# The MLP of a four-layer fp32 trunk on one core: products in program order, high weight tiles first, and a lead that alternates between two blocks

## The chip, the core and the metric

The kernel runs on one core of one Trainium2 chip. The metric is the device time of one execution in microseconds (us). The engines speak through semaphores: PE is TensorE (matmul), ACT is ScalarE, DVE is VectorE, POOL is GpSimd, and SP issues most of the DMAs. Each works through its own instructions in the order in which they stand.

## The reference, cut to what matters

Two layers on 512 tokens of width 1024; each is a mixer (MLA in the first, GLA in the second) followed by an MLP:

```python
x = x + mix
x = x + sq_relu_mlp(rms_norm(x, norm_mlp[i]), mlp_w_up[i], mlp_w_down[i])

def sq_relu_mlp(xn, w_up, w_down):          # w_up 1024 x 4096, w_down 4096 x 1024
    hid = jnp.square(jax.nn.relu(xn @ w_up))
    return hid @ w_down
```

At the end stands one more RMSNorm. The change concerns the two MLPs and the norm ahead of each.

## The kernel before

**Arithmetic.** Every fp32 operand is split into a high and a low fp32r tile (`split`, L108 to L113): ACT copies `src` to `hi` (L110), which rounds, and DVE takes `lo = src - hi` (L113). A product is three matmuls (`mm3`, L118 to L120): high weight by high input, high weight by low input, low weight by high input. `piece` (L143) splits a weight tile; its tiles `wh` and `wl` have three buffers each.

**The products.** Both matmuls of the MLP are cut once in each of three ways (tokens in halves of TH = 256, input width and output width in halves), and seven products are made from sums of the parts where eight would be plain (Strassen's scheme in Winograd's form). The names are 11 and 21 (plain leading part, plain trailing part), T1 to T4 (inputs that are sums of parts of x), and 22. For the up projection the sums of x are made once, by `QuadNorm.pair` (L281), in the output projection ahead of the MLP: for each k of 0 to 3 one ACT operation (L287), four DVE operations (L288 to L291) into a `raw` tile, and a split into `T{k}h` and `T{k}l`. The sums of the weights are made in place on DVE, ahead of each product that needs one (L884, L899, L905, L912).

**Up blocks.** The 4096 hidden columns come in NB = 8 blocks of 512. `up_block(b)` gives the steps s1 (product 11), s5 (T1), s2 (21), s6 (T2), s3 (22), s7 (T3), s4 (T4); block 0 has them in the order 11, 21, T1, T2, 22, T3, T4, behind an s0 that splits its first two weights during the output projection. A product here is 24 matmuls of 128x128 by 128x256: four k, two column groups j, three each, into one PSUM bank (tag `u`, three buffers). The results build on each other in PSUM: T2, T3 and T4 of a block add into one bank (`b2`, tag `seed`, one buffer), which begins as a copy of product 11 (L873); after T3 DVE reads that bank (L915) before T4 may add to it; after T1 and after T2 ACT copies the banks to `mt` tiles (L888, L902). `finish` (L840, L841) multiplies by the norm's 1/rms (`rstd`) and squares. `rstd` is made by `Norm.finish` (L251): a mean by PE (L253), Ln and Exp on ACT, three steps on DVE (L216, L218, L219).

**Down blocks.** `down_block(s)` makes seven products for every pair of up blocks (all but the last pair): 48 matmuls each, in two halves with a `piece` each, into two PSUM banks (tag `d`). The steps of up and down alternate.

**The order.** A scheduler at build time orders each engine's instructions by dependence and priority; so a product's matmuls may stand between those of another. Two calls bind it: `tc.keep_in_program_order(i)` keeps an instruction where the program has it, and `with tc.issue_after(i)` puts the instructions of a block behind `i` on i's engine.

**The lead.** The output projection's last step runs `nxt.pair(3)` (L785). Then `mlp` runs the first two steps of blocks 0 and 1 (L1099 to L1103): 11(0), `begin()` with the norm's mean and four DVE subtractions of x (L1080), 21(0), 11(1), 21(1); the number in brackets is the block. Then come the other steps of block 0, then those of block 1, and so on. Block 1's first weights come as one 1 MB load (L824) into a tile of the pool `down_w`, all others as 512 KB loads (L829) into `raw` tiles of the pool `up` (five buffers).

## Time and profile before

| | |
|---|---|
| median of 3 runs | 1093.47 us (1093.22 to 1094.63) |
| the profiled execution's own time | 1092.46 us |
| its span (first to last instruction) | 1090.7 us |
| busy: PE, DVE, ACT | 1065.7, 892.1, 641.0 us |
| granted clock of PE, mean | 0.996 |
| HBM read, written | 105.69 MB, 2.10 MB |

How to read the profile: rows of the timeline have a start, a duration, engine, line, operation, what is written from what, shapes and a count; square brackets give the idle time ahead and what ended it. Buffer numbers are left out of tile names. Matmuls are pipelined: their durations overlap, and the distance from start to start is the rate. A line is often a helper's, so that L110 and L113 are all splits.

### The profile page before, as it was taken

The page shows a single profiled execution, that of the slowest core. Times are in us where ns is not written, and L with a number is a line of the kernel's source. Part 1 is how long each engine was busy: PE and PEld are TensorE (multiplying, and loading weights), DVE is VectorE, ACT ScalarE, POOL GpSimd, SP SyncE. Part 2 cuts the span into 40 slices and gives each one's busy share as a digit, 9 for nine tenths or more (in the row PEclk, how much of TensorE's full clock was granted, in tenths as well). Part 3 has the DMA queues.
Part 4 walks back from the last instruction along what each step waited for, and adds up shares of the span by engine and source line. Part 5 has one row for each costly group of instructions (what it writes and reads, how often), then busy time and mean ns, then how long its engine had stood idle before and what let it go on. Part 6 is the DMA issues. An engine that isn't in the chain of part 4 may idle for free.

```text
span 1090.7 us, 17825 instructions
## 1 busy us (share of the span) xinstructions
PE 1065.7 (98%) x7322; PEld 981.1 (90%) x7322; DVE 892.1 (82%) x1210; ACT 641.0 (59%) x934; POOL 46.6 (4%) x78
## 2 busy tenths in 40 slices
PE   8999999899999999999999999999999999999997
PEld 6788888889999999998788888887999999999986
DVE  6789878899899899977565655678899899799865
ACT  6577655555667677654334735655565666766734
POOL 6400000000000000030000000000000000000000
PEclk9999999999999999999999999999999999999999
DMA  7312113633433422251222222125424424522312
GB/s 215 87 49 78 29 32 92 198 97 117 149 104 98 155 97 97 78 190 42 53 73 78 78 78 63 53 78 173 132 65 132 141 78 133 167 71 94 134 41 78
DMA packets 99057, 108.93 MB, mean 100 GB/s; under 512 B 8112, under 2 KB 73920, under 8 KB 98976
## 3 DMA queue, kind: packets, MB, share of 16 engines
q1 hardware_dynamic: 96960, 106.57, 31.0%
q10 hardware_dynamic: 1952, 1.21, 0.4%
q8 instruction: 57, 0.93, 0.4%
q0 software_dynamic: 64, 0.02, 0.1%
q14 instruction: 24, 0.20, 0.1%
HBM read 105.69 MB, written 2.10 MB: 99 GB/s over the span
## 4 chain that ended last, share of the span: by engine, by line
PE 87%; DVE 8%; ACT 2%; issue 1%; DMA 1%; SPq 0%; ACTq 0%; DVEq 0%
PE ps L118 27%; PE ps L120 27%; PE ps L119 26%; DVE wl L113 2%; PE ps L135 2%; PE ps L1345 2%; ACT wh L110 1%; DMA wraw_ckv<-in_mla_w_in_dram 1%; DVE raw L1000 1%; DVE raw L884 1%; DVE h L113 0%; PE ps L1382 0%; PE ps L666 0%; DVE raw L912 0%; PE ps L667 0%
## 5 line engine op out<-in xcount | busy, mean ns | idle before, releaser
L110 ACT ACTIVATE wh<-raw 128x1024 fp32r<-128x1024 f32 x210 | 221.3, 1057 | 177.4 <-PE ps L119 135.9
L113 DVE TENSOR_TENSOR wl<-raw,wh 128x1024 fp32r<-128x1024 f32 x210 | 254.4, 1218 | 25.4 <-ACT wh L110 24.9
L120 PE MATMUL ps<-h,wl 128*128 128x256 f32 x672 | 188.4, 280 | 2.6 <-DVE wl L113 2.5
L118 PE MATMUL ps<-h,wh 128*128 128x256 f32 x672 | 187.9, 280 | 0.0
L119 PE MATMUL ps<-h,wh 128*128 128x256 f32 x672 | 187.8, 280 | 0.0
L120 PEld LDWEIGHTS ps<-h,wl 128*128 128x128 f32 x672 | 126.5, 188 | 3.8 <-DVE wl L113 3.8
L118 PEld LDWEIGHTS ps<-h,wh 128*128 128x128 f32 x672 | 126.3, 188 | 0.0
L119 PEld LDWEIGHTS ps<-h,wh 128*128 128x128 f32 x672 | 126.3, 188 | 0.0
L118 PE MATMUL ps<-set,wh 128*128 128x512 f32 x232 | 91.4, 395 | 1.3 <-ACT set L243 1.3
L119 PE MATMUL ps<-set,wh 128*128 128x512 f32 x232 | 90.8, 391 | 1.0 <-DVE set L244 1.0
L120 PE MATMUL ps<-set,wl 128*128 128x512 f32 x232 | 90.6, 390 | 0.0
L110 ACT ACTIVATE wh<-wraw 128x1024 fp32r<-128x1024 f32 x41 | 43.0, 1056 | 73.9 <-PE ps L120 41.5
L118 PE MATMUL ps<-wh,set 128*128 128x512 f32 x144 | 59.7, 414 | 0.0
L841 ACT ACTIVATE q<-q 128x512 f32<-128x512 f32 x64 | 40.1, 627 | 32.0 <-DVE q L840 31.9
L113 DVE TENSOR_TENSOR wl<-wraw,wh 128x1024 fp32r<-128x1024 f32 x41 | 50.0, 1222 | 10.6 <-ACT wh L110 10.5
L113 DVE TENSOR_TENSOR h<-q,h 128x1024 fp32r<-128x1024 f32 x42 | 51.2, 1218 | 7.5 <-ACT h L110 7.5
L120 PE MATMUL ps<-wh,set 128*128 128x512 f32 x144 | 56.4, 391 | 0.0
L119 PE MATMUL ps<-wl,set 128*128 128x512 f32 x144 | 56.2, 391 | 0.0
L119 PEld LDWEIGHTS ps<-set,wh 128*128 128x128 f32 x232 | 43.6, 188 | 11.0 <-DVE set L244 2.2
L118 PEld LDWEIGHTS ps<-set,wh 128*128 128x128 f32 x232 | 43.5, 188 | 11.0 <-ACT set L243 2.0
L120 PEld LDWEIGHTS ps<-set,wl 128*128 128x128 f32 x232 | 43.6, 188 | 8.9
L110 ACT ACTIVATE h<-q 128x1024 fp32r<-128x1024 f32 x42 | 44.1, 1050 | 1.3 <-DVE q L986 1.3
(490 smaller groups left out, 3003.9 us busy)
## 6 DMA issues: line engine op xcount, KB each, us to landing
raw<-in_mlp_w_down_dram SPq DMA_DIRECT2D x38, 1024.0 KB, 5.2
raw<-in_mlp_w_up_dram SPq DMA_DIRECT2D x62, 512.0 KB, 3.8
wraw<-in_gla_w_in_dram SPq DMA_DIRECT2D x11, 1024.0 KB, 5.2
wraw<-in_mla_w_o_dram SPq DMA_DIRECT2D x8, 512.0 KB, 4.8
wraw<-in_gla_w_o_dram SPq DMA_DIRECT2D x8, 512.0 KB, 4.9
raw<-in_mlp_w_up_dram SPq DMA_DIRECT2D x2, 1024.0 KB, 7.7
xT<-in_x_dram SPq DMA_DIRECT2D x6, 256.0 KB, 7.6
wraw_qn<-in_mla_w_uq_dram SPq DMA_DIRECT2D x6, 256.0 KB, 3.4
```

What stands on the lines that cost most here:

```text
L110: order(ACT.activation(hi, src, AF.Copy))
L113: lo_eng.tensor_tensor(lo, src, f(hi), ALU.subtract)
L118: PE.matmul(psum, wh, xh, start=start, stop=False, **kw)
L119: PE.matmul(psum, wh, xl, start=False, stop=False, **kw)
L120: PE.matmul(psum, wl, xh, start=False, stop=stop, **kw)
L135: PE.transpose(psum, src, ident[: src.shape[0], : src.shape[0]])
L841: ACT.activation(qs, qs, AF.Square)
L884: DVE.tensor_tensor(s, v["a21"], v["a22"], ALU.add)
L1000: DVE.tensor_tensor(v["S"], v["12"], v["S"], ALU.subtract)
L1345: PE.matmul(p[:, t * 64 : (t + 1) * 64].rearrange("p (n c) -> p n c", c=m), k[:, sl], later, start=True, stop=True)
```

## The change

1. `matmuls` (L797) no longer calls `mm3`. It issues all high-weight matmuls of the product (16 of 24 in an up product), then the low-weight ones (8), with the two column groups of each k next to each other, and keeps the first matmul in program order, so that products no longer mix.
2. The lead is written anew: 11(0), 11(1), mean, 21(0), 21(1), then blocks 0 and 1 one after the other. Block 1's first weights come as two 512 KB loads of one tile, issued ahead of all further up loads.
3. The sums T for k = 3 are made inside the lead, in a `q` tile, behind the split of block 1's first weight on DVE (`combine`, `combined`); the mean is a method of its own, kept in order.
4. The four subtractions of x stand behind the last weight split of block 0.
5. Two pads move tiles in SBUF.

```diff
...
+    raised, cut_at = [], []
+
...
-            order(ACT.activation(hi, src, AF.Copy))
+            raised.append(order(ACT.activation(hi, src, AF.Copy)))
...
-        lo_eng.tensor_tensor(lo, src, f(hi), ALU.subtract)
+        return lo_eng.tensor_tensor(lo, src, f(hi), ALU.subtract)
...
-        split(raw, hi, lo, order=order)
+        cut_at.append(split(raw, hi, lo, order=order))
...
-            self.acc = None
+            self.acc = self.ms = None
...
+        def mean(self):
+            self.ms = bank("c")
+            return PE.matmul(self.ms, self.inv, self.acc, start=True, stop=True)
+
...
-            m = bank("c")
-            PE.matmul(m, self.inv, self.acc, start=True, stop=True)
+            if self.ms is None:
+                self.mean()
+            m = self.ms
...
+            self.combined(k, self.combine(k, pool.tile([P, 4, TH], F32, tag="raw", bufs=5, name=uname("raw"))))
+
+        def combine(self, k, t):
...
-            t = pool.tile([P, 4, TH], F32, tag="raw", bufs=5, name=uname("raw"))
...
+            return t
+
+        def combined(self, k, t):
+            pool = pool_of("up")
...
-            split(t, hi, lo)
-            for i in range(4):
-                self.quad[f"T{i + 1}"][k] = cut((hi, lo), slice(None), i)
+            i = split(t, hi, lo)
+            for n in range(4):
+                self.quad[f"T{n + 1}"][k] = cut((hi, lo), slice(None), n)
+            return i
...
-            nxt.pair(c)
+            if c < 3:
+                nxt.pair(c)
...
-            for k in ks:
-                for m in ms:
-                    mm3(
-                        p[:, m * TH : (m + 1) * TH],
-                        cut(w, slice(None), k - k0, slice(m * P, (m + 1) * P)),
-                        x[k],
-                        begin and k == 0 and m % 2 == 0,
-                        end and k == 3,
-                        skip_group_check=True,
-                    )
+            def one(i, j, k, m, start, stop):
+                return PE.matmul(
+                    p[:, m * TH : (m + 1) * TH],
+                    w[i][:, k - k0, m * P : (m + 1) * P],
+                    x[k][j],
+                    start=start,
+                    stop=stop,
+                    skip_group_check=True,
+                )
+
+            steps = [(k, m) for k in ks for m in ms]
+            for k, m in steps:
+                i = one(0, 0, k, m, begin and k == 0 and m % 2 == 0, False)
+                if (k, m) == steps[0]:
+                    tc.keep_in_program_order(i)
+                one(0, 1, k, m, False, False)
+            for k, m in steps:
+                one(1, 0, k, m, False, end and k == 3)
...
-                    if not trail:
-                        c0 = b * FB
-                        t = wide_raw().rearrange("p a (b n) -> p (a b) n", b=2)
-                        SP.dma_start(t, w_up[:, c0 : c0 + 256].rearrange("(k p) n -> p k n", p=P))
-                        v["a12"] = t[:, KH:]
-                    return t[:, :KH]
+                    return ahead[trail]
...
-                SP.dma_start(t, w_up[trail * 512 : trail * 512 + 512, c0 : c0 + 256].rearrange("(k p) n -> p k n", p=P))
+                with tc.issue_after(made["load"].ins) if "load" in made else nullcontext():
+                    SP.dma_start(t, w_up[trail * 512 : trail * 512 + 512, c0 : c0 + 256].rearrange("(k p) n -> p k n", p=P))
...
-                for j in range(2):
-                    matmuls(p, w, 0, range(KH), [j], quad[name], begin, True)
+                matmuls(p, w, 0, range(KH), range(2), quad[name], begin, True)
...
-            v = {}
+            v = made[b] = {}
...
-        def begin():
-            nrm.finish()
-            for k in range(KH):
-                DVE.tensor_tensor(xT[k][:, second], xT[k][:, second], xT[k + KH][:, second], ALU.subtract)
-
+        made = {}
...
-        pad(up, PADS["up"])
...
-        opened("down_w")
+        pad(opened("down_w"), PADS["down_w"])
...
-        lead = [blocks[b].pop(0) for b in (0, 0, 1, 1)]
-        for i, step in enumerate(lead):
-            step()
-            if i == 0:
-                begin()
+        t = wide_raw().rearrange("p a (b n) -> p (a b) n", b=2)
+        ahead = t[:, :KH], t[:, KH:]
+        for i, a in enumerate(ahead):
+            made["load"] = SP.dma_start(a, w_up[i * 512 : i * 512 + 512, FB : FB + 256].rearrange("(k p) n -> p k n", p=P))
+        kept = tc.keep_in_program_order
+        made[1]["11"] = piece(ahead[0], KH, 256)
+        with tc.issue_after(raised[-1].ins):
+            blocks[0].pop(0)()
+        blocks[1].pop(0)()
+        with tc.issue_after(cut_at[-1].ins):
+            t = nrm.combine(KH - 1, dp.tile([P, 4, TH], F32, tag="q", bufs=6, name=uname("q")))
+        kept(nrm.mean())
+        made[1]["21"] = piece(ahead[1], KH, 256)
+        kept(cut_at[-1])
+        kept(nrm.combined(KH - 1, t))
+        pad(up, PADS["up"])
+        nrm.finish()
+        for b in range(2):
+            blocks[b].pop(0)()
...
+            if b == 0:
+                with tc.issue_after(cut_at[-1].ins):
+                    for k in range(KH):
+                        DVE.tensor_tensor(xT[k][:, second], xT[k][:, second], xT[k + KH][:, second], ALU.subtract)
...
```

Three places in the order show what the prediction speaks of.

PE in block 0 and block 1 of the first MLP, before: `ps_2552` is the bank of T1(1), `ps_2278` the bank of T2(0) to T4(0), `wh_2516` and `wl_2517` the weights of T4(0).

```order
L119 MATMUL ps_2552<-T3l_2226,wh_2553 128x256
L120 MATMUL ps_2552<-T3h_2225,wl_2554 128x256
L118 MATMUL ps_2552<-T0h_1952,wh_2553 128x256
L119 MATMUL ps_2552<-T0l_1953,wh_2553 128x256
L120 MATMUL ps_2552<-T0h_1952,wl_2554 128x256
L118 MATMUL ps_2278<-T0h_1952,wh_2516 128x256
L119 MATMUL ps_2278<-T0l_1953,wh_2516 128x256
L120 MATMUL ps_2278<-T0h_1952,wl_2517 128x256
```

The same place after: `ps_2275` is the bank of T2(0) to T4(0), `wl_2482` the low weights of T3(0), `wh_2514` the high ones of T4(0).

```order
L814 MATMUL ps_2275<-T2h_2126,wl_2482 128x256 x2
L814 MATMUL ps_2275<-T3h_2318,wl_2482 128x256 x2
L814 MATMUL ps_2275<-T0h_1952,wh_2514 128x256
L814 MATMUL ps_2275<-T0l_1953,wh_2514 128x256
L814 MATMUL ps_2275<-T0h_1952,wh_2514 128x256
L814 MATMUL ps_2275<-T0l_1953,wh_2514 128x256
```

Before, 15 matmuls of T1(1) stand between T3(0) and T4(0), and the low weight follows each pair of high ones. After, T4(0) follows T3(0) directly, and a product's low weights come last.

DVE at the end of the output projection, before: `raw_2219` holds the sums for k = 3, `ps_2280` the mean, `wl_2328` is the low weight of 11(1).

```order
L1080 TENSOR_TENSOR xT<-xT 128x256
L274 SCALAR_TENSOR_TENSOR x7l_2213<-xT,gains,x7h_2212 128x512
L236 TENSOR_TENSOR acc_1936<-acc_1936,tmp_2216 128x512
L289 SCALAR_TENSOR_TENSOR raw_2219<-xT,gains,raw_2219 128x256
L884 TENSOR_TENSOR raw_2251<-raw_2249,raw_2251 128x1024
L290 SCALAR_TENSOR_TENSOR raw_2219<-xT,gains,raw_2219 128x256
L291 SCALAR_TENSOR_TENSOR raw_2219<-xT,gains,raw_2219 128x256
L912 TENSOR_TENSOR raw_2249<-raw_2141,raw_2249 128x1024
L113 TENSOR_TENSOR T3l_2226<-raw_2219,T3h_2225 128x1024
L216 SCALAR_TENSOR_TENSOR mt_2287<-ps_2280,mt_2285 128x512
L218 SCALAR_TENSOR_TENSOR mt_2289<-mt_2287,mt_2285 128x512
L113 TENSOR_TENSOR wl_2328<-raw_2324,wh_2327 128x1024
```

The same place after: `q_2306` holds the sums for k = 3, `ps_2312` the mean, `wl_2241` and `wl_2315` are the low weights of 11(1) and 21(1), `wl_2388` that of T1(0).

```order
L281 SCALAR_TENSOR_TENSOR x7l_2213<-xT,gains,x7h_2212 128x512
L238 TENSOR_TENSOR acc_1936<-acc_1936,tmp_2216 128x512
L115 TENSOR_TENSOR wl_2241<-raw_2237,wh_2240 128x1024
L297 SCALAR_TENSOR_TENSOR q_2306<-xT,gains,q_2306 128x256
L298 SCALAR_TENSOR_TENSOR q_2306<-xT,gains,q_2306 128x256
L299 SCALAR_TENSOR_TENSOR q_2306<-xT,gains,q_2306 128x256
L300 SCALAR_TENSOR_TENSOR q_2306<-xT,gains,q_2306 128x256
L115 TENSOR_TENSOR wl_2315<-raw_2237,wh_2314 128x1024
L902 TENSOR_TENSOR raw_2248<-raw_2246,raw_2248 128x1024
L115 TENSOR_TENSOR T3l_2319<-q_2306,T3h_2318 128x1024
L218 SCALAR_TENSOR_TENSOR mt_2328<-ps_2312,mt_2326 128x512
L115 TENSOR_TENSOR wl_2388<-raw_2248,wh_2387 128x1024
```

The low split of 11(1)'s weight stood behind the sums for k = 3, two weight sums (`raw_2251`, `raw_2249`) and two steps of `rstd`; now it stands ahead of all of these, and the subtraction of x is no longer there.

ACT between block 0 and block 1, before: `wh_2553`, `wh_2586` and `wh_2617` are the high weights of T1(1), T2(1) and 22(1), `ps_2583` is the seed bank of block 1.

```order
L110 ACTIVATE wh_2516<-raw_2514 128x1024
L902 ACTIVATE mt_2448<-ps_2278 128x512
L110 ACTIVATE wh_2553<-raw_2550 128x1024
L841 ACTIVATE q_2248<-q_2248 128x512
L110 ACTIVATE wh_2586<-raw_2550 128x1024
L841 ACTIVATE q_2248<-q_2248 128x512
L110 ACTIVATE wh_2617<-raw_2324 128x1024
L841 ACTIVATE q_2247<-q_2247 128x512
L888 ACTIVATE mt_2581<-ps_2552 128x512
L873 ACTIVATE ps_2583<-mt_2355 128x512
```

The same place after: `wh_2555`, `wh_2588` and `wh_2619` are the high weights of T1(1), T2(1) and 22(1), `mt_2583` is the copy of T1(1)'s result.

```order
L112 ACTIVATE wh_2514<-raw_2512 128x1024
L859 ACTIVATE q_2245<-q_2245 128x512 x2
L112 ACTIVATE wh_2555<-raw_2552 128x1024
L859 ACTIVATE q_2244<-q_2244 128x512
L891 ACTIVATE ps_2585<-mt_2304 128x512
L112 ACTIVATE h_2788<-q_2244 128x1024
L906 ACTIVATE mt_2583<-ps_2554 128x512
L112 ACTIVATE wh_2588<-raw_2552 128x1024
L112 ACTIVATE wh_2619<-raw_2237 128x1024
L112 ACTIVATE wh_2651<-raw_2548 128x1024
```

One squaring stood between the splits of T1(1)'s and T2(1)'s weights; now four operations stand there, the last of which reads T1(1)'s finished bank.

More of the change, by code (lines that the diff above doesn't have):

```diff
@@ L89, in slot @@
         return pool.tile(list(shape), F32R, tag=f"set_{tag}", bufs=16, name=uname("set"))
-    PADS = dict(stage=224, right=64, up=448, masks=256, keep=128)
+    PADS = dict(stage=224, right=64, up=448, masks=256, keep=128, down_w=224)
     def pad(pool, n):
```

## The prediction

> **What bounds the kernel now.** I read the page's busy times and chain first. Then I read the table of windows by stage, PE's waits in the MLP stages, and the rows around them.
>
> ```profile
> PE 1065.7 (98%) x7322; PEld 981.1 (90%) x7322; DVE 892.1 (82%) x1210; ACT 641.0 (59%) x934; POOL 46.6 (4%) x78
> PE 87%; DVE 8%; ACT 2%; issue 1%; DMA 1%; SPq 0%; ACTq 0%; DVEq 0%
> ```
>
> PE works for 98% of the span, so the gain can come only from PE's holes and from PE's rate. The four MLP stages show where the holes are. After "us" the columns are stretch, length, busy time (and instructions) of PE, PEld, DVE, ACT and POOL, granted clock, DMA share and GB/s.
>
> ```profile
> 191.20:242.10 50.90, 45.66 (x364) 43.70 (x363) 46.27 (x50) 28.44 (x36) 0.00 (x0) 0.97 0.48 156
> 242.10:475.90 233.80, 232.02 (x1995) 231.42 (x1995) 219.64 (x200) 156.24 (x177) 5.78 (x8) 1.00 0.35 113
> ...
> 750.20:801.70 51.50, 46.43 (x365) 44.62 (x364) 46.43 (x50) 28.43 (x36) 0.00 (x0) 0.97 0.48 153
> 801.70:1030.00 228.30, 225.75 (x1938) 224.75 (x1937) 213.75 (x194) 150.47 (x170) 0.00 (x0) 1.00 0.35 111
> ```
>
> The first and third rows are the leads: the first 15 products of an MLP (360 matmuls), some 51 us with 5 us idle. The others are the rest of each MLP: 1.8 and 2.5 us idle in some 230. PE's waits in the first lead, then in the rest of the first and second MLP (total, times, longest):
>
> ```profile
> PE ps L118 <- ACT wh L110: 1.8, 2, 0.9
> PE ps L120 <- DVE wl L113: 1.8, 1, 1.8
> PE ps L118 <- ACT mt L888: 1.1, 1, 1.1
> PE ps L118 <- ACT mt L867: 0.5, 1, 0.5
> ```
>
> ```profile
> PE ps L120 <- DVE wl L113: 1.8, 3, 0.8
> ```
>
> ```profile
> PE ps L120 <- DVE wl L113: 2.5, 2, 1.5
> ```
>
> The lead waits for weights and for banks. Later PE waits only for low weights, five times, 4.3 us. DVE is the nearest rival of PE: 219.64 of 233.80 us, 94%.
>
> **The lead: what work alone would take.** PE's rows give the rate of a product:
>
> ```profile
> 191.24 0.28 PE L118 MATMUL ps<-x0h,wh 128*128 128x256 f32 x1
> 193.95 0.28 PE L120 MATMUL ps<-x3h,wl 128*128 128x256 f32 x1
> 195.22 0.28 PE L119 MATMUL ps<-x4l,wh 128*128 128x256 f32 x1
> 199.03 0.38 PE L118 MATMUL ps<-x0h,wh 128*128 128x256 f32 x1 [0.93 <-ACT wh L110]
> 201.28 0.58 PE L120 MATMUL ps<-x0h,wl 128*128 128x256 f32 x1 [1.76 <-DVE wl L113]
> 214.24 0.28 PE L118 MATMUL ps<-x4h,wh 128*128 128x256 f32 x1
> 216.84 0.28 PE L120 MATMUL ps<-x7h,wl 128*128 128x256 f32 x1
> ```
>
> 11(0) takes 23 steps from 191.24 to 193.95, 0.1178 us each, 2.83 for 24. A product from 214.24 to 216.84 takes 0.1130 each, 2.71. The mean lies between 194.07 and 195.10 (one step ahead of 195.22): 1.03. After a wait a matmul lasts 0.38 instead of 0.28, some 0.11 of restart. Four products at 2.83, eleven at 2.71 and the mean are 11.32 + 29.81 + 1.03 = 42.16 us. The lead now takes 50.9 (51.4 in the second MLP), so it loses 8.7 and 9.3: 5.2 us of listed waits, the restarts, and the clock, as the next rows show (columns as above):
>
> ```profile
> 197.30:200.70 3.40, 1.29 (x9) 0.88 (x7) 3.37 (x5) 3.40 (x5) 0.00 (x0) 1.00 0.15 32
> 200.70:204.10 3.40, 2.82 (x13) 2.82 (x14) 3.40 (x5) 0.67 (x2) 0.00 (x0) 0.52 1.05 378
> ...
> 1009.00:1012.40 3.40, 1.86 (x16) 1.65 (x16) 3.40 (x5) 1.51 (x3) 0.00 (x0) 1.00 0.00 0
> ```
>
> PE stood still for 0.93 and 1.76 us with two matmuls between. Behind that the granted clock was 0.52 for 3.4 us, in which 13 matmuls ran instead of some 29: 1.6 us more. In 1009 to 1012.4, with PE busy for 1.86 of 3.40 us, the clock stayed at 1.00. The Trainium skill ("TensorE: Matmul & The Clock Gate", Part 1 and "Why this matters for your kernels") halves the clock after an idle window of about 3.4 us and advises against gaps over about 3 us. This trace lost its clock after two gaps of 0.93 and 1.76 us, neither of which would count by that rule.
>
> **The lead: what it waits for afterwards.** I walk the new order with these durations. ACT and SP:
>
> ```profile
> 186.53 1.04 ACT L110 ACTIVATE wh<-raw 128x1024 fp32r<-128x1024 f32 x1
> ...
> 191.94 0.72 ACT L273 ACTIVATE x7h<-xT,gains 128x512 fp32r<-128x512 f32 x1 [3.05 <-DVE xT L783]
> 192.56 0.62 ACT L235 ACTIVATE tmp<-xT 128x512 f32<-128x512 f32 x1
> ...
> 205.54 0.60 ACT L867 ACTIVATE mt<-ps 128x512 f32<-128x512 f32 x1 [1.32 <-PE ps L120]
> ```
>
> ```profile
> 161.46 26.82 SPq L829 DMA_DIRECT2D raw<-in_mlp_w_up_dram  x4
> 188.44 0.39 SPq L824 DMA_DIRECT2D raw<-in_mlp_w_up_dram  x1
> ```
>
> DVE, and the PE row that ended ACT's wait at 205.54:
>
> ```profile
> 187.80 1.22 DVE L113 TENSOR_TENSOR wl<-raw,wh 128x1024 fp32r<-128x1024 f32 x1
> 188.94 0.48 DVE L274 SCALAR_TENSOR_TENSOR x3l<-xT,gains,x3h 128x256 fp32r<-128x256 f32 x1
> ...
> 202.88 0.68 DVE L840 SCALAR_TENSOR_TENSOR q<-ps,rstd 128x512 f32<-128x512 f32 x1
> 203.48 1.21 DVE L113 TENSOR_TENSOR wl<-raw,wh 128x1024 fp32r<-128x1024 f32 x1
> ```
>
> ```profile
> 205.17 0.28 PE L120 MATMUL ps<-x3h,wl 128*128 128x256 f32 x1
> ```
>
> So a wide split costs ACT 1.04 and DVE 1.22, a 512-wide step 0.60 to 0.72, a bank can be read 0.37 us after its last matmul starts, and the next step begins up to 0.1 before the last one's end (188.94 against 187.80 + 1.22). Times are those of the first MLP.
>
> - 11(1) is free to start at 194.07. Its high split stands on ACT behind x7h (191.94), the square (192.56) and the first sum for k = 3: 193.5 to 194.55. Wait 0.5. The low split follows on DVE (194.6 to 195.8) and is needed after 16 high matmuls (196.6): hidden, where it cost 1.76 before.
> - Mean, 21(0), 21(1), T1(0), T2(0), 22(0), T3(0): no wait. The closest is T2(0), low weight ready at 208.66 and needed at 208.7, then 22(0), whose bank ACT has copied at 208.95, needed at 209.6. The four sums for k = 3 (4 × 0.48) stand on DVE behind 11(1)'s low split; they delay rstd, whose first user, the scaling of 11(0), is off PE's path while three banks last.
> - T4(0) adds to the bank that T3(0) has just filled, and DVE must read it in between. Nothing stands on PE to fill the time, where 15 matmuls of T1(1) did. T3(0) ends at 215.0; the read stands behind a low split and two shorter steps, 215.9 to 216.6. Wait 1.6.
> - T1(1)'s weight sum stands on DVE behind three moved subtractions, 218.1 to 219.3, then ACT splits to 220.4; PE is free at 219.45. Wait 1.0.
> - T2(1)'s weight split stands on ACT behind the copy of T1(1)'s bank. PE ends T1(1) at 223.3, the copy runs 223.5 to 224.1, the split to 225.1. Wait 1.9. Behind it on ACT wait the splits of 22(1) and T3(1), both still early.
> - 22(1), T3(1): none. T4(1) as T4(0), with an idle DVE: free 233.4, read 233.8 to 234.5. Wait 1.1.
> - 11(2) follows; its weight has been split by then.
>
> Sum: 0.5 + 1.6 + 1.0 + 1.9 + 1.1 = 6.1, with five restarts 6.65. The lead comes to 42.16 + 6.65 = 48.8: 2.1 less than 50.9, and 2.6 less than 51.4 in the second MLP. **Term 1: −4.7.** The longest stall, 1.9, is less than the 2.7 of idle that halved the clock, so I add nothing for the clock. Bounds: each of the six handovers is known to about half (±3 per MLP) and may cost a halved clock (1.6 per MLP). The early load of block 1 only moves from 188.44 to the loads that begin at 161.46, onto a queue that is idle then: nothing, and if it stays late that is rival 5. The pads cost nothing: no instruction.
>
> **The rest of the MLPs.** The five later waits look like this one:
>
> ```profile
> 355.51 0.28 PE L119 MATMUL ps<-T0l,wh 128*128 128x256 f32 x1
> 356.60 0.38 PE L120 MATMUL ps<-T0h,wl 128*128 128x256 f32 x1 [0.81 <-DVE wl L113]
> ```
>
> The first low weight is needed as a product's third matmul: 1.09 us from start to start instead of 0.115, which is 0.81 idle and 0.28 of restart. Five of these are 4.3 + 5 × 0.28 = 5.7 us. With the high weights first the low weight is needed as the 17th: 14 × 0.115 = 1.6 us later, more than any of the five (at most 1.5). DVE at 94% has the room to catch up. **Term 2: −5.2**, half a microsecond short of all. Bounds: 0 (the delay comes back elsewhere, rival 4) and −5.7.
>
> **PE's rate.** Afterwards the column groups alternate within a k, so neighbouring matmuls write different halves of the bank. The nearest rows are the down products, which alternate between banks or columns, and GLA products, whose outputs differ too:
>
> ```profile
> 244.86 0.28 PE L118 MATMUL ps<-h,wh 128*128 128x256 f32 x1
> 250.36 0.28 PE L120 MATMUL ps<-h,wl 128*128 128x256 f32 x1
> ```
>
> ```profile
> 612.41 0.28 PE L118 MATMUL ps<-set,ADh 128*128 128x256 f32 x1
> 613.37 0.28 PE L120 MATMUL ps<-set,ADl 128*128 128x256 f32 x1
> ```
>
> 48 matmuls of a down product take 47 steps in 5.50: 0.1170 each. GLA's eight steps in 0.96 are 0.1200. The up products now run at 0.1130 or 0.1178 (above), with the same code: after the lead 233.8 less 2.6 of waits, less 1008 down matmuls at 0.1170, over 984 leaves a mean of 0.1151. Of the 1344 up matmuls of an MLP the bounds are: all at 0.1130, −2.8; at the down products' 0.1170, +2.6; at 0.1178, +3.6. I take +1.0 per MLP, nearer the down rows than the old mean, since the alternation is what they share, but part of the slow rate came behind stalls that go. **Term 3: +2.0** (bounds −5.6 and +7.2). The Trainium skill (the same page, "Back-to-back issue gap" and "LDWEIGHTS") sets the spacing by a matmul and its weight load together, whatever bank they write. Both counts are unchanged at 7322, so by it term 3 would be zero and the forecast 2 us lower.
>
> **Sum.** −4.7 − 5.2 + 2.0 = −7.9. The profiled execution's own time is 1092.46 (span 1090.7 and 1.8 around it), 1.0 under the median 1093.47; so 1084.6 for such an execution and **1085.6** as a median.
>
> **The rivals.**
>
> 1. *The alternation slows every product of the MLP (ends slower).* All 2688 up matmuls and 2016 down matmuls at GLA's 0.1200: 2688 × 0.0049 = 13.2 and 2016 × 0.0030 = 6.0, so −9.9 + 19.2 = +9.3: 1102.8. It decides from a mean of 2.1 ns more per matmul (9.9 / 4704). For it: the rows that alternate are slower than 0.113. Against: the down products alternate already and stand at 0.1170. Chance 0.08.
> 2. *The waits around T3(0) to T2(1) halve the clock in both MLPs.* 1.6 us each, so 1088.8. For it: 1.76 and 0.93 with little between sufficed at 199. Against: here 24 matmuls stand between two waits, and the clock stayed at 1.00 at 1009. Chance 0.10.
> 3. *The handovers cost half of what I walked*, because DVE and ACT run ahead: 3 us less per MLP: 1079.6. For it: ACT is idle for 44% of the lead. Against: the waits after T3 hang on the bank itself. Chance 0.12.
> 4. *The later waits only change their name*: with DVE at 94% the delay returns as waits for high weights, whose sums DVE makes, or for banks. Term 2 is lost: 1090.8. Chance 0.15.
> 5. *Block 1's load does not come early.* It would land 6.7 us after 188.44 at the earliest by the median below, so 11(1) would wait 1.6 more in each MLP: 1088.8. Against: nothing stands ahead of it on SP but two loads. Chance 0.05.
>
> ```profile
> raw<-in_mlp_w_up_dram SPq DMA_DIRECT2D x1, 1024.0 KB, 6.7
> ```
>
> **How the numbers follow.** The forecast has 0.50. A measurement of this kernel can tell about 0.2% from no change, 2.2 us: 1091.3 to 1095.7 count as the same. The forecast's own terms, with the rate between its bounds and the lead within ±3 per MLP, reach from 1077 to 1093. That holds rivals 2 to 5 and leaves out rival 1 and the tails. Faster 0.80: rivals 2, 3 and 5 nearly whole, the forecast but for the rate at its upper bound, and half of rival 4, whose 1090.8 lies at the edge. Same 0.12: the other half of rival 4 and what is left of the forecast. Slower 0.08: rival 1.
>
> **What would show it right or wrong.** In the profile after: the first 15 products of an MLP end 48 to 49 us after the first matmul; no granted clock under 0.9 in the leads; waits of 1 to 2 us on DVE's bank read after T3 and on a high split at T1(1) and T2(1), none on L113-type low splits over 0.3 us later in the MLPs; up products at 0.115 to 0.117 per matmul. Wrong would be: a rate of 0.118 or more throughout, later waits on high splits worth 4 us or more, or a lead over 50 us.

## The result, and the profile after

| | before | after |
|---|---|---|
| median (range) | 1093.57 us (1093.22 to 1094.63) | 1085.97 us (1084.7 to 1087.51) |
| the profiled execution: own time, span | 1092.46, 1090.7 us | 1087.51, 1085.8 us |
| a second profiled execution: own time, span | 1092.94, 1091.2 us | 1085.66, 1083.9 us |

The ratio is 0.9927 (95% interval 0.9914 to 0.994): 7.6 us faster, where 7.9 was forecast. The profiled execution is the slowest of the four that were timed, 1.5 us over their median. The second executions are runs of the same kernels from the experiments.

First the page of the kernel after:

```profile
PE 1063.8 (98%) x7322; PEld 981.4 (90%) x7322; DVE 890.7 (82%) x1210; ACT 640.4 (59%) x934; POOL 44.5 (4%) x78
```

The work is the same to the instruction on PE and DVE. What moved shows in the table of windows, with the bounds at the same products as before: the 15 products of a lead, then the rest of the MLP up to the matmul that follows it.

```profile
191.70:241.00 49.30, 44.61 (x365) 43.14 (x364) 46.46 (x54) 29.83 (x39) 0.00 (x0) 1.00 0.39 126
241.00:474.40 233.40, 233.40 (x1995) 233.30 (x1994) 219.93 (x200) 155.92 (x177) 5.41 (x8) 1.00 0.35 114
748.90:799.20 50.30, 44.60 (x365) 43.13 (x364) 46.45 (x54) 29.97 (x39) 0.00 (x0) 1.00 0.37 123
799.20:1031.30 232.10, 230.68 (x1994) 230.10 (x1993) 219.58 (x199) 155.93 (x178) 0.00 (x0) 1.00 0.36 116
```

The leads are 49.3 and 50.3 us long instead of 50.9 and 51.4, with the clock at 1.00. PE is idle in them about as long as before, 4.7 and 5.7 us against 5.2 and 5.1. In the second row PE is never idle, and yet the stretch is not shorter for it: PE ran slower. PE's waits, in the first lead, in the second, and in the rest of the second MLP (the rest of the first has none):

```profile
PE ps L814 <- ACT wh L112: 2.7, 3, 1.6
PE ps L814 <- DVE q L933: 1.9, 2, 1.2
```

```profile
PE ps L814 <- ACT wh L112: 3.7, 3, 1.6
PE ps L814 <- DVE q L933: 2.0, 2, 1.2
```

```profile
PE ps L814 <- DVE wl L115: 1.4, 2, 1.1
```

No low weight ends a wait in the leads any more. PE's rows give the five waits of the first lead, and the one of 11(1) in the second:

```profile
195.08 0.39 PE L814 MATMUL ps<-x0h,wh 128*128 128x256 f32 x1 [0.35 <-ACT wh L112]
...
217.16 0.36 PE L814 MATMUL ps<-T0h,wh 128*128 128x256 f32 x1 [1.16 <-DVE q L933]
220.98 0.39 PE L814 MATMUL ps<-T0h,wh 128*128 128x256 f32 x1 [0.76 <-ACT wh L112]
225.71 0.39 PE L814 MATMUL ps<-T0h,wh 128*128 128x256 f32 x1 [1.63 <-ACT wh L112]
235.24 0.39 PE L814 MATMUL ps<-T0h,wh 128*128 128x256 f32 x1 [0.78 <-DVE q L933]
...
753.27 0.39 PE L814 MATMUL ps<-x0h,wh 128*128 128x256 f32 x1 [1.36 <-ACT wh L112]
```

They stand where the prediction put them: 11(1), T4(0), T1(1), T2(1), T4(1). The causes are those that it named. ScalarE's rows ahead of 11(1) in the second MLP show why its wait is longer there: the first sum for k = 3 (L296) comes 0.90 us late, behind VectorE's running sum of squares (`acc`), and the split stands behind it.

```profile
751.76 0.51 ACT L296 ACTIVATE q<-xT,gains 128x256 f32<-128x256 f32 x1 [0.90 <-DVE acc L238]
752.17 1.04 ACT L112 ACTIVATE wh<-raw 128x1024 fp32r<-128x1024 f32 x1
```

VectorE's and ScalarE's rows around the second to fourth wait of the first:

```profile
216.00 0.41 DVE L1140 TENSOR_TENSOR xT<-xT 128x256 f32<-128x256 f32 x1
216.33 0.68 DVE L933 TENSOR_TENSOR q<-ps,mt 128x512 f32<-128x512 f32 x1
...
217.87 0.75 DVE L1140 TENSOR_TENSOR xT<-xT 128x256 f32<-128x256 f32 x2
218.54 1.22 DVE L902 TENSOR_TENSOR raw<-raw,raw 128x1024 f32<-128x1024 f32 x1
```

```profile
224.11 0.60 ACT L906 ACTIVATE mt<-ps 128x512 f32<-128x512 f32 x1 [0.36 <-PE ps L814]
224.60 1.05 ACT L112 ACTIVATE wh<-raw 128x1024 fp32r<-128x1024 f32 x1
```

L933 reads the bank of T3(0), and T4(0) starts 0.15 us after it ends. The sum for T1(1) (L902) stands behind the moved subtractions (L1140). The split for T2(1) stands behind the copy of T1(1)'s bank (L906).

The last thing to see is the distance between matmuls in one and the same kind of product, T behind the lead of the first MLP, at 446 and at 457 us (start, duration, count; the down product's first row marks the end):

```profile
446.38 0.28 PE L814 MATMUL ps<-T0h,wh 128*128 128x256 f32 x1
449.21 2.03 PE L814 MATMUL ps<-h,wh 128*128 128x256 f32 x16
...
457.69 0.28 PE L814 MATMUL ps<-T0h,wh 128*128 128x256 f32 x1
...
460.41 2.04 PE L814 MATMUL ps<-h,wh 128*128 128x256 f32 x16
```

24 matmuls take 2.83 us in the first, 2.72 in the second: 0.1179 and 0.1133 each. Up products have these two paces and hardly anything between. In this execution the first MLP kept the long pace from its lead to 452 us, the second the short one from 808 us on but for 907 to 915.

### The profile page after: what moved, and what is told of

Its sections match the earlier page's. It is cut to its first block, busy times and chain, and to the rows that moved or that the text cites. A ratio compares the mean times of both kernels' runs of the same rounds, so it can differ in the third digit from the quotient of the medians.

```text
span 1085.8 us, 17839 instructions
## 1 busy us (share of the span) xinstructions
PE 1063.8 (98%) x7322; PEld 981.4 (90%) x7322; DVE 890.7 (82%) x1210; ACT 640.4 (59%) x934; POOL 44.5 (4%) x78
## 4 chain that ended last, share of the span: by engine, by line
PE 87%; DVE 9%; ACT 2%; issue 1%; DMA 1%; SPq 0%; ACTq 0%; DVEq 0%
PE ps L814 41%; PE ps L120 13%; PE ps L121 12%; PE ps L122 12%; DVE wl L115 3%; PE ps L137 2%; PE ps L1376 2%; ACT wh L112 1%; DMA wraw_ckv<-in_mla_w_in_dram 1%; DVE raw L902 1%; PE ps L1413 0%; DVE q L858 0%; PE ps L680 0%; DVE raw L923 0%; PE ps L681 0%
## 5 line engine op out<-in xcount | busy, mean ns | idle before, releaser
L814 PE MATMUL ps<-h,wh 128*128 128x256 f32 x1344 | 170.8, 279 | 0.0
L814 PEld LDWEIGHTS ps<-h,wh 128*128 128x128 f32 x1344 | 163.0, 188 | 0.0
L814 PE MATMUL ps<-h,wl 128*128 128x256 f32 x672 | 92.4, 280 | 1.1 <-DVE wl L115 1.1
L814 PEld LDWEIGHTS ps<-h,wl 128*128 128x128 f32 x672 | 84.3, 188 | 1.4 <-DVE wl L115 1.3
L814 PE MATMUL ps<-T0h,wh 128*128 128x256 f32 x128 | 33.6, 286 | 8.7 <-ACT wh L112 4.8
L120 PE MATMUL ps<-hh,wh 128*128 128x512 f32 x96 | 37.4, 389 | 0.0
```

Source lines behind the costliest of these rows:

```text
L120: PE.matmul(psum, wh, xh, start=start, stop=False, **kw)
L814: return PE.matmul(p[:, m * TH : (m + 1) * TH], w[i][:, k - k0, m * P : (m + 1) * P], x[k][j], start=start, stop=stop, skip_group_check=True,)
```

## The experiments

Each run gives a median and a profile. The table has every profiled execution, by PE's rows: "lead" is from the first matmul of 11(0) to the first down matmul (one product more than the 15 above), "rest" from there to the first matmul behind the MLP; first MLP / second MLP. "Pace" is that of the up products in the rest.

| | median, us | ratio to before (95%) | leads | rests | pace, us |
|---|---|---|---|---|---|
| before | 1093.57 | 1 | 53.62 / 54.15 | 230.85 / 232.16 | 0.113, 0.118 for about a third of each |
| before, again | (1092.94) | | 54.99 / 52.65 | 231.01 / 232.31 | mostly 0.113 / 0.118 for about a third |
| after | 1085.97 | 0.9927 (0.9914 to 0.994) | 52.08 / 53.09 | 230.54 / 229.30 | 0.118 / 0.113 |
| after, again | (1085.66) | | 51.76 / 53.02 | 228.04 / 230.34 | 0.113 / mostly 0.113 |
| new lead, low between | 1094.96 | 1.0016 (1.0007 to 1.0025) | 53.12 / 56.64 | 230.80 / 232.80 | 0.113 / both |
| high first, old lead | 1082.37 | 0.9896 (0.9882 to 0.9911) | 51.52 / 51.04 | 228.39 / 229.89 | 0.113 / mostly 0.113 |
| the same, again | 1084.84 | 0.9914 (0.9896 to 0.9932) | 51.89 / 50.79 | 228.65 / 230.85 | 0.113 / 0.118 |
| the same, in order | 1087.45 | 0.9938 (0.9923 to 0.9953) | 51.92 / 51.91 | 230.87 / 230.91 | 0.118 / 0.118 |
| in order, again | (1083.97) | | 51.58 / 51.91 | 228.04 / 230.52 | 0.113 / 0.118 |
| columns apart | 1085.53 | 0.9926 (0.9914 to 0.9938) | 52.08 / 53.08 | 228.88 / 230.52 | 0.113 / 0.118 |
| T4 later | 1086.37 | 0.9929 (0.9911 to 0.9948) | 52.30 / 51.67 | 230.54 / 230.89 | 0.118 / 0.118 |
| other places | 1086.04 | 0.9929 (0.9911 to 0.9947) | 51.04 / 52.42 | 228.75 / 229.28 | 0.113 / 0.113 |
| both of these | 1092.92 | 0.9995 (0.9983 to 1.0006) | 56.31 / 54.92 | 231.00 / 231.00 | 0.118 / 0.118 |
| early load, old lead | 1088.24 | 0.9949 (0.9932 to 0.9966) | 52.71 / 53.00 | 228.53 / 231.04 | 0.113 / both |

A time in brackets is a single execution. The kernel before had medians of 1093.54, 1093.70 and 1094.87 us beside the three groups of runs, so kernels of different groups are compared by their ratios.

**Which half of the change works.** Two runs take the change apart: new lead with the old order inside a product, and old lead with the new one. For the first ("new lead, low between") the loops in `matmuls` become the old ones:

```diff
...
-            for k, m in steps:
-                i = one(0, 0, k, m, begin and k == 0 and m % 2 == 0, False)
...
-                one(0, 1, k, m, False, False)
-            for k, m in steps:
-                one(1, 0, k, m, False, end and k == 3)
+            for m in ms:
+                for k in ks:
...
+                    i = PE.matmul(c, wh, xh, start=s, stop=False, skip_group_check=True)
...
+                    PE.matmul(c, wh, xl, start=False, stop=False, skip_group_check=True)
+                    PE.matmul(c, wl, xh, start=False, stop=end and k == 3, skip_group_check=True)
```

> The changed kernel, but each product of the MLPs issues high, high, low weight for each k again, one column group after the other (the scheduler, which follows, orders VectorE's later steps anew). Theory: high weights first is what removed the later waits for low weights, so 4 to 6 us of them come back, and 1 to 2 us per lead where a low split now ends last: 1091 to 1096 us. Rival: the new order on VectorE removed them, not the order within a product: 1085 to 1088 us, and later waits under 2 us in the profile.

Measured 1094.96 us, 1.4 us (0.16%) slower than before. PE's waits in its two leads:

```profile
PE ps L820 <- DVE q L928: 3.0, 2, 1.9
PE ps L825 <- DVE wl L115: 2.2, 2, 1.5
PE ps L820 <- ACT wh L112: 0.4, 1, 0.4
```

```profile
PE ps L820 <- DVE q L928: 3.1, 2, 2.1
PE ps L825 <- DVE wl L115: 1.9, 2, 1.2
PE ps L820 <- ACT wh L112: 1.4, 1, 1.4
```

The low weights are back as releasers (L825), and behind the leads they end three waits, 2.6 us in all, in each MLP. The theory holds; against the kernel after, the leads lose 4.8 us in sum and the rests 4.5.

The second ("high first, old lead") is the kernel before with the new `matmuls`, but without its `keep_in_program_order`, so that products may still mix:

```diff
...
-                for j in range(2):
-                    matmuls(p, w, 0, range(KH), [j], quad[name], begin, True)
+                matmuls(p, w, 0, range(KH), range(2), quad[name], begin, True)
```

> The kernel before with high weights first and alternating columns in each product, old lead, no fixed order between products. Theory: the later waits go (about 5 us) and in the lead the 1.76 us wait for a low weight with the halved clock behind it goes too (up to 3 us per MLP), the other waits of the old lead stay: 1083 to 1088 us, as fast as the changed kernel. Rival: the lead's new order carries the gain of the lead, and the later waits come back as waits for high weights: 1089 to 1093 us.

Measured 1082.37 us, 0.6 under the range of the theory, and 1084.84 in the other group, inside it. Both profiled executions also lost some 1.5 us to a halved clock at 15 us, ahead of the MLPs; that is in their times (1084.54 and 1085.7 us) and not in the table's leads and rests. Its waits in the leads are shorter than those of the new lead:

```profile
PE ps L799 <- DVE q L920: 1.4, 2, 0.9
PE ps L799 <- ACT mt L893: 1.3, 1, 1.3
PE ps L799 <- ACT wh L110: 0.9, 1, 0.9
```

```profile
PE ps L799 <- ACT mt L893: 1.3, 1, 1.3
PE ps L799 <- ACT wh L110: 0.9, 1, 0.9
PE ps L799 <- DVE q L920: 0.7, 1, 0.7
```

The 1.76 us for a low weight and the halved clock behind it are gone without any change of the lead. The table makes a square of four, by sums over both MLPs (means where there are two executions):

| leads, rests | old lead | new lead |
|---|---|---|
| low between | 107.7, 463.2 | 109.8, 463.6 |
| high first | 102.6, 458.9 | 105.0, 459.1 |

High weights first takes 4.8 to 5.1 us from the leads and 4.3 to 4.5 from the rests, with either lead. The new lead adds 2.1 to 2.4 to the leads, with either order, and nothing to the rests. So all of the gain, and more, comes from one half of the change. One restriction: in both runs the scheduler ordered VectorE's and ScalarE's steps anew to suit the products, so "high weights first" includes what it made of that.

**Where the new lead loses.** Two of its parts were put into the old lead one at a time. First the fixed order:

```diff
+                if (k, m) == steps[0]:
+                    tc.keep_in_program_order(i)
```

> The kernel before with the changed products, and these kept in program order (the run with high weights first and the old lead let them mix). Theory A: the fixed order of the products costs the changed kernel its lead, since T4 has to wait for VectorE's read of the bank that T3 fills and nothing fills that time: two waits of about 1 us and their restarts per MLP come back, 1085 to 1087 us. Theory B: the new order of the lead and the places of its weight splits and subtractions cost it: this run stays at 1081.5 to 1083.5 us.

> High weights first, old lead, products in program order once more, for a second profile. If the program decides the pace, both MLPs run at 0.118 throughout again, and the 5 us to the kernel that lets the products mix are mostly pace (944 matmuls per MLP behind the lead by 4.6 ns, 4.3 us); if executions draw it, other stretches show.

The median of 1087.45 us, half a microsecond over its range, would speak for theory A and somewhat more. The profiles put only 1.0 us in the leads (103.8 and 103.5 against 102.6). The first profile had the long pace in both MLPs from end to end, the second the short one in the first MLP, and 1083.97 us. By the ratios the ordered kernel is 2.6 to 4.6 us slower than the two medians of the one that lets products mix. So theory A is right for about 1 us; that the rest is pace fits the two profiles, which are too few to show it. Whether the fixed order makes the long pace likelier is open.

Then the early weights of block 1:

```diff
...
+        for i, a in enumerate(ahead):
+            made["load"] = SP.dma_start(a, w_up[i * 512 : i * 512 + 512, FB : FB + 256].rearrange("(k p) n -> p k n", p=P))
+        made[1]["11"] = piece(ahead[0], KH, 256)
         lead = [blocks[b].pop(0) for b in (0, 0, 1, 1)]
...
```

> The kernel with high weights first and the old lead, with one more part of the change: block 1's first weights come early, in two loads, and 11(1)'s weight is split ahead of 11(0). Theory: the waits of 0.9 us for the high split of 11(1) go from both leads and nothing else moves: 1080 to 1081.5 us. Rival: VectorE and ScalarE only do the same work in another order and the wait returns at the next product: 1082 to 1083.5 us.

> High weights first with the old lead once more, for its times beside the run with the early load and for a second profile. If the program decides which pace the up products get, it shows 0.113 us in most of both MLPs again and 1082 to 1083 us; if every execution draws its pace anew, the stretches move and with them up to 4 us per MLP.

Measured 1088.24 beside 1084.84 us: both expectations of the early load missed, it is 3.4 us slower. Its leads are 105.7 in sum against 102.6. The waits of the first:

```profile
PE ps L799 <- ACT mt L889: 1.7, 1, 1.7
PE ps L799 <- DVE q L916: 1.5, 2, 0.9
PE ps L799 <- ACT wh L110: 1.5, 2, 0.8
PE ps L799 <- ACT mt L868: 0.7, 1, 0.7
```

The wait for a high split became two, and waits for copies of banks (L868, L889) grew from 1.3 to 2.4. My reading is that weights that are split early take their turn on ScalarE and VectorE ahead of steps that the next products need, and that the new lead is longer than the old one by the same kind of exchange; no run shows that apart.

**Can the new lead's waits be moved away?**

"T4 later" changes the order of the steps:

```diff
...
+            if b == 0:
+                blocks[0].insert(-1, blocks[1].pop(0))
+            if b == 1:
+                blocks[1].insert(-1, blocks[2].pop(0))
...
```

> The changed kernel with T1(1) ahead of T4(0) and 11(2) ahead of T4(1) (block 2's first result is kept in a copy until the bank is free, two more copies on ScalarE). Theory: the waits of T4 for VectorE's read (1.9 us and two restarts of 0.17 per MLP) are covered: 1081 to 1083 us. Rival: VectorE, at 94% in the lead, sets the pace and the time returns as waits for weights: 1085 to 1087 us.

Measured 1086.37 us; no gain. Neither reason holds as it was put: T4's wait is covered, but T2(1) then waits for the copy that seeds the bank, as that bank is free only after T4(0):

```profile
225.16 0.38 PE L814 MATMUL ps<-T0h,wh 128*128 128x256 f32 x1 [2.82 <-ACT ps L891]
```

One bank for T2 to T4 of all blocks looks like the limit that the old lead and the new share; no run gave them a second one. The clock fell to 0.50 behind this wait.

"Other places" moves the first sum for k = 3 behind 11(1)'s split, T2(1)'s split ahead of the copy, and the subtractions behind block 1:

```diff
...
-        with tc.issue_after(cut_at[-1].ins):
+        with tc.issue_after(cut_at[-1].ins), tc.issue_after(first_split.ins):
             t = nrm.combine(KH - 1, dp.tile([P, 4, TH], F32, tag="q", bufs=6, name=uname("q")))
...
+                if b == 1:
+                    DVE.tensor_tensor(s, s, v["a11"], ALU.subtract)
+                    v["T2"] = piece(s, KH, 256)
                 v["p5"] = mt()
-                ACT.activation(v["p5"], v["x5"], AF.Copy)
+                with tc.issue_after(raised[-1].ins) if b == 1 else nullcontext():
+                    ACT.activation(v["p5"], v["x5"], AF.Copy)
...
-            if b == 0:
+            if b == 1:
                 with tc.issue_after(cut_at[-1].ins):
```

> The changed kernel with three steps in other places: the first sum for k = 3 behind the split of 11(1)'s weight on ScalarE, the weight split of T2(1) ahead of the copy of T1(1)'s bank, the four subtractions of x behind block 1 instead of block 0. Theory: the waits for high weights in the leads (2.7 and 3.7 us, three each) mostly go, those of T4 stay: 1081 to 1083 us. Rival: VectorE is the bound of the lead and they come back: 1085 to 1087 us.

Measured 1086.04 us. The waits for high splits are all gone, and T4's waits for VectorE have grown from 1.9 and 2.0 to 3.9 and 4.3 us. The leads are 103.5 in sum, 1.5 less than after; the median shows nothing of it. The profiled execution (1083.75 us) is the fastest of six that reach 1088.95; two of the six have a mean granted clock of 0.993, where the kernel after has 0.996 or more, so halved clocks behind the longer waits may take back what the lead gains. VectorE, 94% busy in the lead, seems to give the time to whom it serves first.

> The changed kernel with the edits of the two runs before together. Theory: leads with under 1 us of waits each, 46 to 47 us for 15 products, 1077 to 1080 us, faster than any kernel so far. Rival: VectorE's own 45 to 46 us in the lead leave nothing more than either edit alone gives: 1081 to 1083 us.

Measured 1092.92 us, outside both expectations: leads of 56.3 and 54.9 us, with waits of 2.7 us on a high split and 1.9 on the seed, and the clock halved behind both in the first MLP and behind the second in the other.

**The pace.** "Columns apart" turns the loops round:

```diff
-            steps = [(k, m) for k in ks for m in ms]
+            steps = [(k, m) for m in ms for k in ks]
```

> The changed kernel with the column groups of a product one after the other (all high weights of group 0, then of group 1, then the low ones); the orders on all other engines are unchanged. Prediction's term 3: alternating columns costs about 2 us of rate, so 1083 to 1085 us and up products at 0.113 to 0.115 us per matmul throughout. Rival: the rate is one of two paces, 0.113 and 0.118, that changes at stalls and has nothing to do with columns: 1085 to 1088 us, both paces in the profile.

Measured 1085.53 us (0.9926, 0.9914 to 0.9938), the same as after. The orders on the other engines are those of the kernel after, and both paces show, each for most of an MLP. The rival holds: alternating columns costs nothing that these runs can tell.

> The changed kernel once more, for its profile. If the two paces of the up products (0.113 and 0.118 us per matmul) are a state that an execution falls into, the stretches of each differ from the first profile, where the first MLP ran at 0.118 from 191 to 452 us and the second at 0.113 from 808 us on, and the time moves with them by 4.7 ns per up matmul; if addresses or instructions set them, the same stretches come at the same pace.

1085.66 us. The first MLP, at 0.118 in the first profile, ran at 0.113 from 236 to its end. It is the same program, so nothing in the program decides it. The old lead with high weights first, the ordered version and their second runs show the same. What it is worth stands in the table: a rest at the long pace (but for at most the last 20 us) takes 230.5 to 231.0 us, in ten MLPs under high weights first; one at the short pace for most of the way takes 228.0 to 228.9, in the first MLP of seven runs, and 229.3 in the second MLP of two. That is up to 3 us in the first MLP, 1.2 to 1.7 in the second, and not the 4.4 of the 960 up matmuls behind the lead by 4.6 ns, because PE then runs into VectorE. The second profile of the kernel after, first MLP:

```profile
448.31 1.21 PE L814 MATMUL ps<-h,wl 128*128 128x256 f32 x8 [1.09 <-DVE wl L115]
```

A wait of 1.1 us on a low weight stands in each of the seven at the short pace, two such waits of 1.4 us in all in each of the two, and none in the ten at the long one.

> The kernel before once more, for a second profile. The waits are the same as in the first (5.2 and 5.1 us in the leads, 1.8 and 2.5 us later, within 0.3). The stretches at 0.118 (401 to 458 us, 899 to 962 us and from 1017 us) either stand where they stood, or move.

1092.94 us. Waits as expected but for one (2.8 instead of 1.8 us in the first rest). The stretches of the long pace stand nearly where they were in the second MLP; in the first, the one that had begun at a wait at 404 us began only behind the wait at 452. The clock stayed at 0.50 for two windows in the first lead, from 201.0 to 207.8 us, hence 54.99, and at 1.00 throughout the second lead behind the same two waits (1.03 and 1.75 us), hence 52.65. So what a halved clock costs the old kernel differs from one execution to the next.

## Why the prediction was right in the time, and where not

The sum came out at −7.9, measured −7.6. It is the right number with all three terms off, and that is luck: term 1 promised 2.0 us too much and terms 2 and 3 together 0.9 too little. The leads and rests give −6.8 in the profiled executions; the medians differ by 7.6, since both profiled executions of the kernel before lie under its median.

Of the prediction's own signs some failed. The first 15 products took 49.3 and 50.3 us instead of 48 to 49, and the second is over the 50 that it called wrong. The up products ran at 0.118 in the first MLP up to 452 us, a pace that it called wrong if it held throughout, and mostly at 0.113 in the second; 0.115 to 0.117 was nowhere to be seen. One later wait on a low split was 1.1 us, not under 0.3. The full clock in the leads and the absence of later waits on high splits came as forecast.

**What bounds it, and the second rival's clock.** Right: PE's holes and PE's rate are all that changed. The forecast took no halved clock in the leads; it stayed at 1.00 in all four leads of the kernel after.

**Term 1, the leads: −4.7, measured −2.7** (107.7 to 105.0, two executions each). The walk put every wait at its place and cause, and in the first MLP each a little too long: 0.35 for 0.5, 1.16 for 1.6, 0.76 for 1.0, 1.63 for 1.9, 0.78 for 1.1; 4.7 for 6.1 in all. Three other steps failed. "11(1) ... wait 0.5" holds for the first MLP only: in the second, ScalarE's first sum for k = 3 began 0.90 us late and the split behind it with it, 1.36. "Eleven at 2.71": the up products of the leads ran at 0.118 for the most part, 2.83 a product, which is 1.3 us per MLP. And "some 0.11 of restart": around T1(1)'s wait of 0.76 us, PE's starts at 219.95, 220.98 and 221.20 us are 1.03 and 0.22 apart instead of 0.118 each, 0.27 beside the wait itself, so five restarts cost 0.8 us more per MLP than the sum has. (Behind the lead the prediction counted 0.28 for the same thing, which is near.)

**What the term is made of.** The prediction gave the gain of the lead to its new order together with the late low weights. The square shows two terms of opposite sign: high weights first −4.8 to −5.1, the new order +2.1 to +2.4. The step that the prediction lacked is the comparison with the old lead under high weights first: it counted the new lead's waits (6.1) against the old lead's waits as they stood (5.2) and the clock, though the 1.76 us wait on a low weight and the clock behind it fall by themselves once the low weight is needed 14 matmuls later. The rule for the later waits (term 2) was there; inside the new lead it was used ("hidden, where it cost 1.76 before"), but the old lead was not priced with it alone.

**Term 2, the later waits: −5.2; terms 2 and 3 together −3.2, measured −4.1** (the rests, 463.2 to 459.1). That the order inside the product removes them is shown by the first run. They do not go wholly: a wait of 1.1 us on a low weight of a down product remains where PE runs at the short pace. The −4.1 also holds what each execution drew as its pace, so terms 2 and 3 can't be told apart to better than that.

**Term 3, the alternation: +2.0, shown wrong in its reason.** The 0.117 of the down products does not come from alternating columns: with columns apart they average 0.1172 and 0.1167 in the two MLPs, in the kernel after 0.1167 and 0.1171. The paces of the up products are 0.113 and 0.118 with and without alternation. The size, between −5.6 and +7.2, held what an execution may draw, up to 3 us per MLP, but not for the reason given. The Trainium skill's rule ("TensorE: Matmul & The Clock Gate", "Back-to-back issue gap" and "LDWEIGHTS") gave zero, and for columns the run agrees: 1085.53 against 1085.97 us.

**The rivals.** The first fell (no product at 0.120 over an MLP). The second did not happen in the kernel after, but in its relatives with waits of 1.9 to 2.8 us. The third was right in part: the waits were a quarter shorter than walked in the first MLP and 7% in the second. The fourth, later waits that change their name, fell: what remains in the kernel after, up to 1.6 us per MLP, still waits for low weights. The fifth fell: block 1's loads were issued at 164 us. It is the split, not the load, that came late.

## What to carry to other kernels

If a product needs a split operand, issue the part that is ready first for the whole product, and the late part last: it moved each low weight's due time by 14 matmuls and gave 9 to 10 of 1094 us in leads and rests, with either lead. When a change has two halves, price each against the kernel that has the other half already; waits that the first half removes are no longer there for the second to save. In these leads, with VectorE 94% busy, the new orders that were tried mostly chose who waits.

## What the hardware showed that was not expected

- **Two paces for one instruction stream.** Pairs of weight load (128x128) and matmul (128x256) follow each other at 0.1133 or at 0.1179 us, for up to 230 us on end. By PE's starts in the 14 traces, of 147 places where a wait stands between two stretches of up matmuls, the pace changes at 46. Stretches of down matmuls without a wait ran at 0.117, or, 27 times, at 0.120, and behind each of these 27 the up products went from the long pace to the short one. The same program drew different paces in all four pairs of executions. What sets it was not found.
- **A halved clock after one wait, or not.** In the run with other places, T4(0) waited 2.23 us in both MLPs, up to 771.66 and up to 217.33 us. The windows around both waits, second MLP first (the granted clock stands third from the end):

```profile
768.48:771.89 3.41, 1.18 (x11) 1.01 (x10) 3.41 (x5) 1.49 (x2) 0.00 (x0) 1.00 0.77 207
771.89:775.30 3.41, 3.41 (x18) 3.41 (x18) 3.38 (x4) 0.83 (x2) 0.00 (x0) 0.50 0.30 105
215.47:218.88 3.41, 1.55 (x13) 1.58 (x14) 3.41 (x5) 1.69 (x2) 0.00 (x0) 1.00 0.77 233
218.88:222.29 3.41, 3.41 (x33) 3.41 (x32) 3.38 (x5) 1.50 (x2) 0.00 (x0) 1.00 0.00 2
```

  The same wait halved the clock for 3.4 us once and not at all the other time. The bounds of these windows are not free: the trace records the granted clock in steps of 3.413 us that keep their phase for a whole execution (in the kernel before, the halvings begin at 200.80 and 760.59 us, 164 steps apart). Counted back from 771.89, the second MLP's wait lies whole in one step, while a border at 215.47 us cuts the first one's and leaves 1.8 us in the step behind it. In the MLPs of the 14 traces each of the nine steps with 1.9 us or more of idle PE is followed by a step at 0.50. Of the seven with 1.6 to 1.8 us one is (1.65 us, new lead with low between), and of those with less, at full clock, none. A longer wait stays free where a border divides it: 2.57 us in T4 later, second MLP. The Trainium skill ("TensorE: Matmul & The Clock Gate", Part 1) describes a window of 3.4 us that runs freely, whatever the kernel does. That fits these borders; its figure of 3.4 us of idle does not fit a loss after 1.9 to 2.8. Why the clock stayed at 0.50 for a second step once (kernel before, again) is open.
